# A hybrid encoder layer on one core: sequence mixers stepped between dense products, exponents as sums of clamped differences, and low parts of weights kept in DRAM

## The chip, the cores and the metric

The kernel runs on one core of a Trainium2 chip. The metric is the device time of one execution in microseconds (us), the median of several runs. The engines are named as the profile names them: PE (TensorE), its weight loads PEld, DVE (VectorE), ACT (ScalarE), POOL (GpSimd) and SP (SyncE, whose queue issues all DMAs of this kernel).

## What is computed

One encoder layer is applied to two independent streams with the same weights: S with 512 tokens and R with 1024, both of width 1024 in float32. Cut to what matters here:

```python
u = rmsnorm(x) @ w_in                      # 3088 columns: z, x/B/C, dt, q, k, v
ssd = gated_norm(scan_fwd(...) + scan_bwd(...) + D * xs, silu(z))
att = rmsnorm(dilated_attention(rope(norm(q)), rope(norm(k)), v))
h = x + concat(ssd, att) @ w_out
h = h + cross_attention(rmsnorm(h), rmsnorm(mem))          # 4 heads, 256 memory tokens
y = h + relu(rmsnorm(h) @ w1) ** 2 @ w2
...
# scan, per chunk of 128 tokens, head and direction
seg = a_cs[i] - a_cs[j]                    # a_cs: running sum of dt * A, A < 0
lmat = where(causal, exp(seg), 0)
y_diag = (C @ B.T * lmat) @ (x * dt)
y_off = (C @ carried_state) * exp(a_cs)
```

## The kernel before

**Dense products in three parts.** A float32 product is made of three fp32r products: both factors are split into a rounded high part and a rest, and `mm3` (lines 180 to 183) adds high x high, low x high and high x low. `load_w` (line 163) brings a slab of weights as two halves `raw` of 0.5 MB over SP's queue; ACT rounds each half into `whi` (line 172), and the rest `wlo` is a subtraction (line 173), of the first half on POOL and of the second on DVE. There are two `raw` buffers and three of `whi` and `wlo`. Each slab of `w_in` (12 of them, 256 columns each) is loaded and split once for S and again for R.

**The order of the work.** The program records the stages one after another: norm and `w_in` of S, scan of S (`ssd`), norm of R's first half, q/k/v of S (`w_in_qkv`), attention of S (`att`), norm and `w_in` of R, scan of R, q/k/v of R, attention of R, the keys and values of the memory tokens (`memory`), then `chain` (w_out and cross attention) and `mlp` of S, and the same two of R. A scheduler then orders each engine's instructions: of those whose inputs and buffers it holds to be ready, the one recorded first goes first. So a later stage's dense products already stand between the steps of a mixer that waits. Each engine, and the SP queue, runs its own instructions strictly in that order.

**The scan** (line 463 on). A backward pass makes the states that come from the right and stores them in DRAM. The forward pass takes chunk by chunk (128 tokens): it loads x, B, C, z and the stored state, makes C.B for two groups of heads in PSUM bank b (line 542) and masks it for both directions (DVE, line 545). For each of two groups of four heads it loads rows `se` of the running sums, broadcast to all partitions (line 551), and forms the exponent as the smaller of the two directions' differences:

```python
nc.scalar.activation(e[:, 0, h], e[:, 0, h], AF.Identity, bias=col[0])                       # line 555
nc.vector.scalar_tensor_tensor(e[:, 0, h], w[:, h], col[1], e[:, 0, h], op0=OP.add, op1=OP.min)   # 556
```

Lines 557 and 558 weigh the masked C.B with dt (ACT and DVE), 559 takes Exp (ACT), 560 multiplies (POOL), and 563 applies the result to x in bank c. Two products with the carried states follow (line 573, both in bank b, read by DVE at 575 into `syo`), and the state's own product (line 513, bank b again).

**q, k and v** (line 401 on). For each slab and each pair of token tiles two projections of 24 products each (256 columns) are copied out by ACT (line 448). For q and k, `heads` squares, sums, takes a reciprocal root on POOL (line 190), scales and rotates (DVE and POOL, 421 to 428), and transposes on PE (line 433).

**Attention** (line 619 on). Four pairs of heads; per head a band pattern and a class pattern; units of two query tiles. A unit is scores in bank a (line 653), the mask and maximum on DVE (655), Exp on ACT (660), transposes in bank b (666), a copy, and values in bank c (676).

## Time and profile before

| | |
|---|---|
| three runs | 2495.92, 2488.87, 2497.25 us; median 2495.92 |
| the profiled execution | 2489.01 us, span of its instructions 2487.2 us |
| mean granted clock of TensorE | 0.993 |
| busy, share of the span | PE 97%, DVE 56%, ACT 38%, POOL 28% |
| DMA | 272.6 MB in all |

An instruction's line in the profile is the line of the function that records it: all dense products stand under lines 181 to 183, and the name of the tile tells them apart (`mm` and `tp` are banks of dense products and transposes, `ma`, `mb`, `mc` the three banks of the mixers). A name ends in s or p where it belongs to S or R (`acs`, `acp`). The span falls into stretches by what runs: up to about 70 us the start and w_in of S, to 212 the scan of S with q/k/v of S, to 447 attention of S with w_in of R, to 756 the scan of R with q/k/v of R and the memory products and the first part of attention R, to 1132 the rest of attention R with memory and the chain of S, and from there the MLP of S and all else of R.

### The profile page before, as it was taken

Reading aid. Unit: us, or ns where it says so; the run is one execution under the profiler, and the core shown is the slowest. Engines: PE = TensorE matmul, PEld = TensorE weight load, DVE = VectorE, ACT = ScalarE, POOL = GpSimd, SP = SyncE. Lnnn points to the kernel's source line nnn. Section 1 sums busy time; section 2 is a strip of 40 time slices with the busy share of each in tenths; the row PEclk is TensorE's granted clock in tenths of the full one; section 3 lists DMA queues with packets and bytes.
Section 4 is the critical chain, followed back from the end, with each engine's and each line's share of the span. In section 5 each row is a group of like instructions: output and inputs, shape, how many; then the busy total and the mean of one; then the engine's idle time right before and its main releaser. Section 6 shows DMA issues by size and latency. Waiting matters only on the chain.

```text
span 2487.2 us, 43450 instructions
## 1 busy us (share of the span) xinstructions
PE 2419.2 (97%) x17363; PEld 2268.0 (91%) x17363; DVE 1394.9 (56%) x2750; ACT 951.3 (38%) x2153; POOL 698.4 (28%) x492
## 2 busy tenths in 40 slices
PE   8989999999989999999999999999999999999999
PEld 8889999889889988999989999999989989989897
DVE  6896775787735666655445636445544444443444
ACT  6655554455544655543222315334412212112120
POOL 3363112564422221314334211111222222122220
PEclk9999999999999999999999999999999999999999
DMA  5755443765567253425233411111111111101101
GB/s 187 243 192 181 126 146 106 225 201 189 187 194 214 85 150 98 116 83 184 92 101 103 170 52 35 52 60 44 35 52 35 51 52 51 52 35 52 52 35 68
DMA packets 224059, 272.59 MB, mean 110 GB/s; under 512 B 39634, under 2 KB 178160, under 8 KB 223856
## 3 DMA queue, kind: packets, MB, share of 16 engines
q1 hardware_dynamic: 223856, 269.80, 34.1%
q8 instruction: 137, 2.24, 0.4%
q14 instruction: 66, 0.54, 0.1%
HBM read 215.55 MB, written 54.20 MB: 108 GB/s over the span
## 4 chain that ended last, share of the span: by engine, by line
PE 79%; DMA 6%; DVE 6%; issue 3%; POOL 2%; ACT 2%; SPq 1%; POOLq 0%; DVEq 0%; ACTq 0%
PE mm L181 16%; PE mm L183 16%; PE mm L182 16%; PE tp L183 7%; PE tp L182 7%; PE tp L181 7%; PE mc L676 2%; PE ma L653 2%; PE mb L666 1%; DMA se<-acp 1%; DVE wlo L173 1%; PE tp L199 1%; DVE se L558 1%; POOL wlo L173 1%; DMA ak<-qkp 1%
## 5 line engine op out<-in xcount | busy, mean ns | idle before, releaser
L181 PE MATMUL mm<-whi,chi 128*128 128x256 f32 x1792 | 516.6, 289 | 2.1 <-ACT mm L749 1.2
L183 PE MATMUL mm<-whi,clo 128*128 128x256 f32 x1792 | 512.2, 287 | 0.0
L182 PE MATMUL mm<-wlo,chi 128*128 128x256 f32 x1792 | 511.3, 286 | 0.0
L947 DVE TENSOR_TENSOR h<-mm,h 128x512 f32<-128x512 f32 x384 | 262.2, 689 | 408.6 <-PE mm L183 408.6
L173 POOL TENSOR_TENSOR wlo<-raw,whi 128x1024 fp32r<-128x1024 f32 x120 | 296.9, 2474 | 601.4 <-ACT whi L172 585.9
L183 PE MATMUL tp<-chi,wlo 128*128 128x256 f32 x1440 | 408.4, 284 | 0.0
L182 PE MATMUL tp<-clo,whi 128*128 128x256 f32 x1440 | 407.9, 283 | 0.0
L181 PE MATMUL tp<-chi,whi 128*128 128x256 f32 x1440 | 405.6, 282 | 0.0
L172 ACT CAST whi<-raw 128x1024 fp32r<-128x1024 f32 x240 | 241.7, 1047 | 293.1 <-PE mm L183 168.1
L181 PEld LDWEIGHTS mm<-whi,chi 128*128 128x128 f32 x1792 | 341.1, 190 | 4.5 <-ACT chi L205 1.7
L182 PEld LDWEIGHTS mm<-wlo,chi 128*128 128x128 f32 x1792 | 341.0, 190 | 1.2 <-issue 0.2
L183 PEld LDWEIGHTS mm<-whi,clo 128*128 128x128 f32 x1792 | 339.9, 190 | 0.4
L173 DVE TENSOR_TENSOR wlo<-raw,whi 128x1024 fp32r<-128x1024 f32 x120 | 265.8, 2215 | 108.5 <-ACT whi L172 108.2
L181 PE MATMUL mm<-whi,hidh 128*128 128x512 f32 x768 | 303.1, 395 | 0.2 <-DVE h L947 0.2
L182 PE MATMUL mm<-wlo,hidh 128*128 128x512 f32 x768 | 302.6, 394 | 0.0
L183 PE MATMUL mm<-whi,hidl 128*128 128x512 f32 x768 | 302.3, 394 | 0.2 <-POOL hidl L932 0.2
L181 PEld LDWEIGHTS tp<-chi,whi 128*128 128x128 f32 x1440 | 272.5, 189 | 8.7
L183 PEld LDWEIGHTS tp<-chi,wlo 128*128 128x128 f32 x1440 | 271.7, 189 | 7.0
L182 PEld LDWEIGHTS tp<-clo,whi 128*128 128x128 f32 x1440 | 270.9, 188 | 6.5
L932 POOL TENSOR_TENSOR hidl<-hr,hidh 128x512 fp32r<-128x512 f32 x96 | 133.3, 1390 | 473.6 <-ACT hidh L931 473.6
L931 ACT CAST hidh<-hr 128x512 fp32r<-128x512 f32 x96 | 59.5, 620 | 320.6 <-PE mm L182 249.6
L183 PEld LDWEIGHTS mm<-whi,hidl 128*128 128x128 f32 x768 | 144.3, 188 | 34.0 <-POOL hidl L932 0.6
(283 smaller groups left out, 4398.3 us busy)
## 6 DMA issues: line engine op xcount, KB each, us to landing
raw<-in_mlp_w_dram SPq DMA_DIRECT2D x128, 512.0 KB
raw<-in_w_in_dram SPq DMA_DIRECT2D x48, 512.0 KB
qkp<-ev SPq DMA_DIRECT2D x32, 256.0 KB
se<-acp SPq DMA_DIRECT2D x16, 512.0 KB
raw<-in_xatt_wkv_dram SPq DMA_DIRECT2D x16, 512.0 KB
ak<-qkp SPq DMA_DIRECT2D x32, 256.0 KB
raw<-in_w_out_dram SPq DMA_DIRECT2D x16, 512.0 KB
raw<-in_xatt_wq_dram SPq DMA_DIRECT2D x16, 512.0 KB
```

The source lines that it names most:

```text
L172: nc.scalar.copy(hi[:, sl, :], raw)
L173: (nc.vector if s else nc.gpsimd).tensor_tensor(lo[:, sl, :], raw, f(hi[:, sl, :]), op=OP.subtract)
L181: nc.tensor.matmul(ps, lh, rh, start=start, stop=False)
L182: nc.tensor.matmul(ps, lh, rl, start=False, stop=False)
L183: nc.tensor.matmul(ps, ll, rh, start=False, stop=stop)
L199: nc.tensor.transpose(pt[:, k, t, :], xn[t][:, (2 * kp + k) * 128:(2 * kp + k + 1) * 128], units(2 * kp + k))
L558: nc.vector.scalar_tensor_tensor(w[:, h], cbm[:, 0, g], col[2], w[:, h], op0=OP.mult, op1=OP.add)
L653: nc.tensor.matmul(pq[:, i, :W], qu, ops[i][0][j], start=j == 0, stop=j == 1)
L676: nc.tensor.matmul(po[:, i * 64:i * 64 + 64], pT[:, i * nk + j, :], ops[i][1][j][:, rs], start=j == 0, stop=j == nk - 1)
L931: nc.scalar.copy(hh[:, ft], r)
L932: nc.gpsimd.tensor_tensor(hl[:, ft], r, f(hh[:, ft]), op=OP.subtract)
L947: nc.vector.tensor_tensor(h[t][:, cs], ps, h[t][:, cs], op=OP.add)
```

## The change

**Kept rests.** `load_w` takes a key, which only slabs of w_in have. The first time a slab with a key is split (for S), both halves of the rest are made by POOL and the whole rest is stored to DRAM; the second time (for R) it is loaded from there instead of being made again. Other weights are split as before.

**Exponents.** The exponent is minus the sum of the two directions' differences, each clamped at zero by a Relu on ACT; POOL adds them, and ACT takes Exp with scale -1.

**Weaving.** The stages become generators that yield after a step: a mixer after a part of a chunk or a unit, a dense stage after one projection bank or pair of tiles. `weave` takes `rate` mixer steps for each dense step, so the recorded order itself alternates. In the scan, the loads, the masks and the weights of chunk c+1 are recorded during chunk c, the state's product and one of the two products with carried states use bank a. In q/k/v the transposes of a pair of tiles are recorded after the next pair's projections; in `xbc` those of the convolution likewise. In attention a unit's scores, transposes and values are recorded in three successive steps, so three units are under way. Attention R is woven into `memory`, `chain` of S and `mlp` of S.

```diff
+    def load_w(src, a, b, key=None):
...
+            if kept is not None:
+                nc.sync.dma_start(f(lo[:, sl, :]), kept[:, sl, :])
+            else:
+                eng = nc.gpsimd if key or s == 0 else nc.vector
+                eng.tensor_tensor(lo[:, sl, :], raw, f(hi[:, sl, :]), op=OP.subtract)
+        if key and kept is None:
+            rests[key] = tc.dram_tile([128, a, b], F32, name="rest%d" % len(rests))
+            nc.sync.dma_start(rests[key], f(lo))
...
-                    nc.scalar.activation(e[:, 0, h], e[:, 0, h], AF.Identity, bias=col[0])
-                    nc.vector.scalar_tensor_tensor(e[:, 0, h], w[:, h], col[1], e[:, 0, h], op0=OP.add, op1=OP.min)
...
+        def weigh(c, g, cbm, e):
+            w = e[:, 1]
+            for h in range(4):
+                for d in range(2):
+                    col = acs[:, c, d * 8 + g * 4 + h:d * 8 + g * 4 + h + 1]
+                    nc.scalar.activation(e[:, d, h], e[:, d, h], AF.Relu, scale=-1.0, bias=col)
+            nc.gpsimd.tensor_tensor(e[:, 0], e[:, 0], w, op=OP.add)
+            nc.scalar.activation(e[:, 0], e[:, 0], AF.Exp, scale=-1.0)
+            for h in range(4):
+                col = [st.dt[:, c, d * 8 + g * 4 + h:d * 8 + g * 4 + h + 1] for d in range(2)]
+                nc.scalar.activation(w[:, h], cbm[:, 1, g], AF.Identity, scale=col[1])
+                nc.vector.scalar_tensor_tensor(w[:, h], cbm[:, 0, g], col[0], w[:, h], op0=OP.mult, op1=OP.add)
+            nc.gpsimd.tensor_tensor(w, w, e[:, 0], op=OP.mult)
...
+        def outside(c, d, prev, y):
...
+            po = mx_bank("ab"[d])
...
+            inside(c, 0, py)
+            if nxt:
+                tiles[c + 1] = load(c + 1, True)
+                e0 = rows_of(c + 1, 0)
+                xs = decayed(x, c, 0)
+            yield
+            inside(c, 1, py)
+            if nxt:
+                cbm = masks(c + 1)
+                e1 = rows_of(c + 1, 1)
             nc.vector.tensor_tensor(y, py, y, op=OP.add)
+            outside(c, 0, carry, y)
+            yield
+            if nxt:
+                weigh(c + 1, 0, cbm, e0)
+            outside(c, 1, pb, y)
...
+            yield
+            if nxt:
+                carry = update(carry, xs, bt, c, 0)
+                weigh(c + 1, 1, cbm, e1)
...
+                if behind:
+                    transposed(*behind.pop())
                 if c < 4:
                     heads(c, t, hl)
+                    behind.append((c, t, hl))
...
+    def weave(mixer, rate, dense):
+        due = 0.0
+        for _ in dense:
+            due += rate
+            while due >= 1.0:
+                due -= 1.0
+                next(mixer, None)
...
+            mixer = ssd(S, mp)
+            weave(mixer, 1.5, w_in_norm(R, pool, atB, 0))
+            rot = rotations(pool)
+            weave(mixer, 1.7, w_in_qkv(S, pool, rot))
+            run(mixer)
...
+            mixer = att(S, mp)
+            weave(mixer, 1.6, w_in_norm(R, pool, atA, 1))
+            weave(mixer, 1.6, w_in(R, pool, wx))
+            run(mixer)
...
+            mixer = ssd(R, mp)
+            weave(mixer, 1.8, w_in_qkv(R, pool, rot, lambda: memory_norm(pool, atB)))
+            run(mixer)
...
+        mixer = att(R, att_pool.__enter__())
+        weave(mixer, 1, memory(pool, lambda: [mix_T(S, pr, atA) for pr in range(2)]))
...
+        weave(mixer, 1, chain(S, (atA,), hp, tp_only))
...
+            weave(mixer, 1, mlp(S, hid, lambda: [run(mixer)] + [mix_T(R, pr, atA) for pr in range(2)]))
```

Three places of the orders that the two programs get show what moves.

On SP's queue, at the second and third slab of w_in in S's pass (`raw` is half a slab, `wd` the columns of dt), before:

```order
L171 DMA raw_470<-in_w_in_dram 128x4x256
L171 DMA raw_474<-in_w_in_dram 128x4x256
L346 DMA wd_4053<-in_w_in_dram 128x8x16
L171 DMA raw_620<-in_w_in_dram 128x4x256
L171 DMA raw_624<-in_w_in_dram 128x4x256
```

and after the change:

```order
L175 DMA raw_464<-in_w_in_dram 128x4x256
L184 DMA rest0_254<-wlo_245 128x2048
L175 DMA raw_468<-in_w_in_dram 128x4x256
L371 DMA wd_3273<-in_w_in_dram 128x8x16
L175 DMA raw_616<-in_w_in_dram 128x4x256
L184 DMA rest1_472<-wlo_463 128x2048
L175 DMA raw_620<-in_w_in_dram 128x4x256
```

The store of a slab's rest stands between the two loads of the next slab; it waits for POOL's second subtraction, as the load behind it does, which takes that half's buffer.

On PE, in the scan of R, one chunk from its products with carried states to the next chunk's masks ("..." stands for dense products, `tp` for q/k transposes), before:

```order
L573 MATMUL mb_5931<-carry_5850,sbc_5867 128x256 x2
...
L563 MATMUL mc_5879<-sx_5863,se_5880 128x64 x4
L573 MATMUL mb_5937<-spb_5871,sbc_5867 128x256 x2
L563 MATMUL mc_5879<-sx_5863,se_5904 128x64 x4
...
L513 MATMUL mb_5945<-sxs_5943,sbt_5865 128x256 x2
...
L542 MATMUL mb_5971<-sbc_5965 128x128 x2
```

and after the change:

```order
L551 MATMUL ma_6954<-sxs_6819,sbt_6482 128x256 x2
...
L607 MATMUL mc_6806<-sx_6480,se_6577 128x64 x4
L616 MATMUL mb_6946<-spb_6804,sbc_6484 128x256 x2
L616 MATMUL ma_7098<-carry_6957,sbc_6815 128x256 x2
...
L463 MATMUL tp_7158<-tab_75,ev_6990 128x128 x4
...
L576 MATMUL mb_7089<-sbc_7079 128x128 x2
L463 MATMUL tp_7297<-tab_75,ev_7105 128x128 x4
L607 MATMUL mc_7070<-sx_6811,se_6817 128x64 x4
```

All four products of a chunk other than the inner one used bank b in turn; now two of them use bank a, and the product with the carried state already belongs to the next chunk.

On POOL, in the same scan (`rsr` is a reciprocal root, `ev` a rotation of q or k, `se` a group's exponents and weights), before:

```order
L560 TENSOR_TENSOR se_5684<-se_5684 128x512
L565 TENSOR_TENSOR sy_5830<-sx_5765,rowt_76 128x512
L560 TENSOR_TENSOR se_5708<-se_5708 128x512
L190 TENSOR_TENSOR rsr_7365<-rst_7363,nhalf_79 128x8
L426 TENSOR_TENSOR ev_7306<-ev_7307,rot_1705 128x64 x2
L576 TENSOR_TENSOR sy_5732<-sy_5732,syo_5738 128x512
```

and after the change:

```order
L594 TENSOR_TENSOR se_6229<-se_6229 128x512
L452 TENSOR_TENSOR ev_6613<-ev_6614,rot_1326 128x64 x2
L594 TENSOR_TENSOR se_6320<-se_6320 128x512
L557 TENSOR_TENSOR carry_6693<-carry_6440,sdec_5579 128x512
L600 TENSOR_TENSOR se_6229<-se_6229 128x512
L202 TENSOR_TENSOR rsr_6793<-rst_6791,nhalf_79 128x8
L619 TENSOR_TENSOR sy_6214<-sy_6214,syo_6345 128x512
L600 TENSOR_TENSOR se_6320<-se_6320 128x512
```

Each group now has two operations there, the sum (line 594) and the product (line 600), and others stand between them.

## Rows read from the trace of the kernel before

**Rows 1.** The page: span, and PE's busy time, share and instructions.

```profile
span 2487.2 us, 43450 instructions
...
PE 2419.2 (97%) x17363; PEld 2268.0 (91%) x17363; DVE 1394.9 (56%) x2750; ACT 951.3 (38%) x2153; POOL 698.4 (28%) x492
```

**Rows 2.** Busy time in one stretch of 50 us; columns as in rows 3.

```profile
200.00:250.00 50.00, 50.00 (x433) 49.28 (x433) 30.44 (x92) 30.02 (x76) 10.60 (x11) 1.00 0.53 173
```

**Rows 3.** Busy time by stretch: from:to, length, then the header's columns.

```profile
core 0: us, PE busy (x) PEld busy (x) DVE busy (x) ACT busy (x) POOL busy (x), PEclk, DMA share, GB/s
0.00:70.00 70.00, 60.38 (x487) 58.56 (x488) 48.22 (x109) 41.59 (x71) 20.05 (x19) 1.00 0.61 194
70.00:212.00 142.00, 130.08 (x1014) 126.05 (x1013) 120.67 (x241) 79.93 (x187) 77.32 (x63) 0.96 0.66 214
212.00:447.00 235.00, 232.36 (x1986) 230.20 (x1985) 152.97 (x446) 121.68 (x319) 50.48 (x41) 1.00 0.45 136
447.00:756.00 309.00, 280.63 (x2178) 271.08 (x2178) 212.24 (x479) 155.30 (x420) 147.24 (x125) 0.97 0.63 200
756.00:1132.00 376.00, 366.81 (x2790) 347.48 (x2789) 224.95 (x576) 193.07 (x515) 97.08 (x57) 1.00 0.42 120
1132.00:2487.00 1355.00, 1348.93 (x8920) 1234.65 (x8918) 635.82 (x903) 359.68 (x645) 306.22 (x188) 1.00 0.19 66
```

**Rows 4.** Waits of PE over the span: total us, times, longest.

```profile
PE tp L433 <- DVE ev L428: 11.9, 7, 3.2
...
PE ma L653 <- DMA ak<-qkp: 5.4, 3, 2.8
PE mb L573 <- DVE syo L575: 5.1, 2, 4.4
PE ma L653 <- DVE aband L655: 4.3, 4, 2.7
```

**Rows 5.** Stretches at half clock: the first of seven, and their sum.

```profile
82.00:88.60 6.60, 4.76 (x18) 4.23 (x19) 6.58 (x20) 4.52 (x15) 0.00 (x0) 0.50 0.58 212
...
sum 28.20, PE 25.86 PEld 23.94 DVE 18.72 ACT 10.39 POOL 9.06; mean PE 3.69 PEld 3.42 DVE 2.67 ACT 1.48 POOL 1.29
```

**Rows 6.** Line 173 alone, by stretch: DVE busy, POOL busy, clock, DMA.

```profile
70.00:212.00 142.00, 16.38 (x9) 22.21 (x9) 0.96 0.66 214
...
447.00:756.00 309.00, 22.61 (x12) 30.72 (x12) 0.97 0.63 200
```

**Rows 7.** Line 173: durations of one, ns, minimum/median/maximum, and first and last start.

```profile
L173 POOL TENSOR_TENSOR wlo<-raw,whi x120: 2347/2407/3412, 13.1 to 2422.7; 128x1024 fp32r<-128x1024 f32 x120
L173 DVE TENSOR_TENSOR wlo<-raw,whi x120: 1154/2522/3407, 15.1 to 2423.3; 128x1024 fp32r<-128x1024 f32 x120
```

**Rows 8.** Groups: busy us, mean ns of one | idle before, releasers.

```profile
L190 POOL TENSOR_TENSOR rsr<-rst,nhalf 128x8 f32<-128x8 f32 x25 | 42.4, 1695 | 38.5 <-DVE rst L188 37.9
L556 DVE SCALAR_TENSOR_TENSOR se<-se,sa 128x128 f32<-128x128 f32 x96 | 35.7, 415 | 9.8 <-ACT se L555 9.7
L560 POOL TENSOR_TENSOR se<-se 128x512 f32<-128x512 f32 x24 | 32.3, 1350 | 14.6 <-DVE se L558 12.0 <-issue 1.0 <-PE mc L563 0.8
L555 ACT ACTIVATE se<-se,sa 128x128 f32<-128x128 f32 x96 | 30.7, 390 | 33.8 <-DMA se<-acp 26.6 <-DMA se<-acs 5.6 <-POOL ev L426 1.6
```

**Rows 9.** Line 556 alone, by stretch: DVE busy, clock, DMA.

```profile
70.00:212.00 142.00, 11.50 (x32) 0.96 0.66 214
...
447.00:756.00 309.00, 24.18 (x64) 0.97 0.63 200
```

**Rows 10.** Waits of PE in 70 to 212 us, the longest three.

```profile
PE tp L433 <- DVE ev L428: 5.3, 3, 2.1
PE tp L199 <- DVE sdd L478: 2.7, 1, 2.7
PE ma L483 <- DVE sacs L474: 1.8, 1, 1.8
```

**Rows 11.** Waits of PE in 447 to 756 us, the longest.

```profile
PE tp L433 <- DVE ev L428: 6.7, 4, 3.2
```

More of the change, by code (lines that the diff above doesn't have):

```diff
@@ L167, in load_w @@
         h = a // 2
+        kept = rests.get(key)
         for s in range(2):
@@ L385, in steps @@
             nc.vector.scalar_tensor_tensor(st.dt, q, 2.0, v, op0=OP.mult, op1=OP.add)
+            yield
         for part, i in ((xbc, 0), (steps, 0), (xbc, 1), (xbc, 2), (xbc, 3), (gate, 0), (gate, 1)):
-            part(i)
+            yield from part(i)
     def rotations(pool):
@@ L458, in w_in_qkv @@
                     mid()
+                yield
     def ssd(st, pool):
@@ L525, in ssd, with masks @@
             x, bt = load(c, False)
[L526 removed]
+            xs = decayed(x, c, 1)
+            yield
+            carry = update(carry, xs, bt, c, 1)
             nc.sync.dma_start(st.pb[c - 1], carry)
[L529 to L539 removed]
+        tiles, weights = {}, {}
+        def masks(c):
+            bc = tiles[c][2]
             pcb = mx_bank("b")
@@ new lines, in inside @@
+        def inside(c, g, py):
+            w, x = weights.pop((c, g)), tiles[c][0]
+            for h in range(4):
+                hs = slice((g * 4 + h) * 64, (g * 4 + h) * 64 + 64)
+                nc.tensor.matmul(py[:, hs], w[:, h], x[:, hs], start=True, stop=True)
+        def outside(c, d, prev, y):
+            if prev is None:
+                return
+            bc = tiles[c][2]
+            po = mx_bank("ab"[d])
+            for g in range(2):
+                gs = slice(g * 256, g * 256 + 256)
+                nc.tensor.matmul(po[:, gs], bc[:, 2 + g, :], prev[:, gs], start=True, stop=True)
+            t = pool.tile([128, 512], F32, name="syo", bufs=1)
+            nc.vector.tensor_tensor(h3(t), h3(po), bc64(eacs[:, c, d * 8:d * 8 + 8]), op=OP.mult)
+            nc.gpsimd.tensor_tensor(y, y, t, op=OP.add)
@@ L564, in ssd @@
+        tiles[0] = load(0, True)
+        yield
+        carry = None
+        cbm = masks(0)
+        for g in range(2):
+            weigh(0, g, cbm, rows_of(0, g))
+            yield
+        for c in range(nt):
+            nxt = c + 1 < nt
+            sl = slice(c * 128, c * 128 + 128)
+            x, bt, bc = tiles[c]
             y = pool.tile([128, 512], F32, name="sy", bufs=2)
             nc.gpsimd.tensor_tensor(h3(y), h3(x), bc64(Dsk), op=OP.mult)
-            nc.vector.tensor_tensor(y, py, y, op=OP.add)
@@ L567, in ssd @@
-            for d in range(2):
-                if prev[d] is None:
-                    continue
-                po = mx_bank("b")
-                for g in range(2):
-                    gs = slice(g * 256, g * 256 + 256)
-                    nc.tensor.matmul(po[:, gs], bc[:, 2 + g, :], prev[d][:, gs], start=True, stop=True)
-                t = pool.tile([128, 512], F32, name="syo", bufs=1)
-                nc.vector.tensor_tensor(h3(t), h3(po), bc64(eacs[:, c, d * 8:d * 8 + 8]), op=OP.mult)
-                nc.gpsimd.tensor_tensor(y, y, t, op=OP.add)
@@ L683, in part, with step @@
                     nc.sync.dma_start(out[r], no[:, i])
+            return [(u0, (scores, transposed, values)) for u0 in range(0, nt, 2)]
+        flying = []
+        def step(unit):
+            if unit:
+                flying.append((*unit, 0, ()))
+            for i, (u0, stages, n, r) in enumerate(list(flying)):
+                flying[i] = (u0, stages, n + 1, stages[n](u0, *r))
+            if flying and flying[0][2] == 3:
+                flying.pop(0)
         for h in range(2):
@@ L687, in att_pair @@
             for classes in (False, True):
-                part(h, classes, qs, ks)
+                for unit in part(h, classes, qs, ks):
+                    step(unit)
+                    yield
+        while flying:
+            step(None)
+            yield
         cls = pool.tile([128, nt, 2, 66], F32, name="acl", bufs=1)
@@ L957, in mlp, with run @@
             nc.sync.dma_start(st.y[t * 128:t * 128 + 128, :], h[t])
+    def run(gen):
+        for _ in gen:
+            pass
+    def weave(mixer, rate, dense):
[5 more added lines that the diff above has]
+                next(mixer, None)
     tp_only = lambda tag: tp_bank()
@@ L975, in hm @@
             st.hm.append(norm_h(st, pr, pools[pr // 2], "mlp_norm_g", banks))
-        w_out(st, hp, hn)
+        yield from w_out(st, hp, hn)
         with tc.tile_pool(name="xa" + st.tag, bufs=1, reuse_waits="tile") as xp:
-            xattn(st, xp, xp, bank, lambda: hn(last), hm)
+            yield from xattn(st, xp, xp, bank, lambda: hn(last), hm)
     with ExitStack() as es:
```

150 lines of the change are left out of this document (75 added, 75 removed).

## The prediction

> **What bounds the kernel now.** I read the views in this order: busy shares, the table of stretches, the waits of TensorE, and the groups on the lines that the change touches. PE is busy 2419.2 of 2487.2 us [rows 1], so only what keeps PE from its next product counts. An undisturbed stretch runs 433 matmuls in 50 us [rows 2], 0.116 us each; nothing in the change alters how many dense products there are, so that part stays. The stretches [rows 3] show where PE is kept waiting. Its idle time is 142 - 130.1 = 11.9 us in 70 to 212 (the scan of the short stream S between its q/k/v products), 2.6 in 212 to 447 (attention S, w_in of R), 28.4 in 447 to 756 (the scan of R, then the start of attention R) and 9.2 in 756 to 1132 (attention R between memory and chain S): 52.1 us together. In the first stretch DVE is busy 120.7 of 142 us, 85%; in the third 212.2 of 309, the most loaded engine after PE in both. From 1132 on, no mixer runs and PE idles 6.1 us in 1355. The waits [rows 4] name the same places: the q/k transposes behind DVE's rotation 11.9 us, the scan's one PSUM bank b behind DVE 5.1, the score products behind their loads of K 5.4 and behind DVE 4.3. [...]
>
> **The change, part by part.** The sum stands against the profiled execution, 2489.0 us, span 2487.2. The three runs shown have a median of 2495.9, from 2488.9 to 2497.3, so the profiled one lies at their low end.
>
> *Kept rests.* Twelve slabs of w_in are used by S and again by R. In S's pass DVE loses its 12 halves to POOL; in R's pass the 24 subtractions go, and 24 loads of 0.5 MB come; 12 stores of 1 MB are new in S's pass. Of these DVE loses 9 in 70 to 212, 16.4 us, and POOL, which has 9 of its own there, gains 9 x 2.41 = 21.7 [rows 6, 7]. In R's q/k/v products both lose about 5 of the 12 halves shown in 447 to 756: 5/12 of 22.6 and 30.7 us, 9.4 on DVE and 12.8 on POOL [rows 6]. The stores bring 12.6 MB into the first 212 us, 59 GB/s above 194 and 214 at a DMA share of 0.61 and 0.66 [rows 3]; in proportion the share rises to about 0.83. Below 1 I cost this at 1 us, with bounds of 0 (the weights are three buffers deep) and 10 (a late half slab of 48 products, 5.6 us, twice). The store waits on the SP queue for POOL's second half, and behind it stands the raw load that waits for the same subtraction anyway; the next loads of the scan stand further back, and they are what pays if POOL is late. At the very start, the first slab's second half now waits for the first on POOL, 2.4 us, where DVE took it alongside: 1 us, bounds 0 and 2.4.
>
> *Exponents.* Per group of four heads, 4 DVE operations of 0.37 us busy go (96 in all, 35.7 us: 11.5 and 24.2 in the two scans [rows 8, 9]), 4 more ACT operations of 0.32 come, and one more POOL operation like the 1.35 us product. POOL's sum now stands in the middle of the chain: ACT, POOL, ACT and DVE, POOL.
>
> *The loads that result.* In 70 to 212 DVE goes from 120.7 to 120.7 - 16.4 - 11.5 = 92.8, 65%; POOL from 77.3 to 77.3 + 21.7 + 8 x 1.35 = 109.8, 77%, and is the most loaded there; ACT reaches 79.9 + 10.2, 63%. In 447 to 756 DVE goes to 212.2 - 9.4 - 24.2 = 178.6, 58%; POOL to 147.2 - 12.8 + 21.6 = 156, 50%; ACT to 155.3 + 20.5 = 176, 57%. No engine beside PE keeps 85%.
>
> *Weaving: scan.* A chunk's exponent rows are loaded half a chunk before ACT needs them; before, ACT sat idle 26.6 + 5.6 us behind these loads [rows 8]. The state product and one of the two outer products move from bank b to bank a, so a chunk uses bank b twice instead of four times, and the 5.1 us behind syo lose their cause. The q/k transposes stand after the next pair of projections in the code, but counted in the scheduler's order this is less: 98 dense products behind their own projection on average, 85 before, so 13 x 0.116 = 1.5 us more cover, while the waits were 7 of 1.7 us on average. Of the 11.9 us in 70 to 212, where three waits ended by DVE make 9.8 [rows 10], I take 7: DVE has a quarter less to do, but POOL now feeds the same chains; bounds 0 and 11.9. Of the 28.4 in 447 to 756 I take 13: bank b 5.1, half of the transposes' 6.7 there [rows 11], and 4.6 of the smaller DVE waits; bounds 0 and 25.
>
> *Weaving: attention.* Scores, transposes and values of a unit are three steps apart, and attention R is spread from the memory products into the MLP of S, so that more dense products lie between its parts. The loads of K and q are issued as before. Of the 2.6 + 9.2 us I take 5, bounds 0 and 10.
>
> [...]
>
> *The sum.* 7 + 13 + 5 + 7 - 1 - 1 = 30 us, 2489 - 30 = 2459 us for a run like the profiled one. The median of runs lay 6.9 us above it before, so I put the median of the changed kernel at **2460**.
>
> [...] DVE's subtraction takes 1154 ns at best and 2522 in the median, up to 3407, while POOL's stays at 2347 to 3412 with a median of 2407 [rows 7]: something in POOL's half makes DVE's half wait. [...]
>
> **The rivals.**
> [...]
> - *The order hardly changes.* The scheduler wove already: 85 against 98 products. Then attention's 5 us, the transposes' 3.3 and half of the clock term go: 2459 + 12 = 2471.
> - *POOL takes DVE's place.* 77% on an engine whose operations last 1.35 to 2.4 us, with the reciprocal roots of q and k in the same queue. Then scan S wins nothing, scan R only bank b (13 becomes 5), the clock 2: 2459 + 7 + 8 + 5 = 2479, the median near 2486.
> - *Slower: ACT stands behind POOL's sum.* The Exp waits at the head of ACT's queue for the new sum, and the copies that free the three PSUM banks of the dense products queue behind it. A bank lasts 24 products, 2.8 us, so PE stalls once ACT is held for more than two banks, 5.6 us. With a subtraction (2.4), a sum of the other group (1.35), one root (1.7 us [rows 8]) and the sum itself (1.35), POOL's queue holds 6.8: 1.2 us too long, and 24 groups make 29 us, with nothing won in the scans or the clock: 2489 - 5 + 2 + 29 = 2515. Against it: subtractions are gone in R's pass, and the scheduler places other ACT work ahead of the Exp.
>
> **How the numbers follow.** Forecast 0.50, port 0.08, order 0.15, POOL 0.17, slower 0.10. The range reaches from 2432, where the large terms come near their upper bounds and the costs to nothing (11 + 23 + 9 + 14 = 57 us below 2489), to 2492, which holds the first four cases with the 7 us between the profiled run and the median; it leaves out the slower case and the far end of the gain, some 0.15 together. A measurement of this kernel can tell about 0.3%, 7.5 us. Faster by more: the first three cases and a little of the fourth, 0.76; within 0.3%: 0.14; slower: 0.10.
>
> **What would show it.** DVE busy falls by some 80 us (24 subtractions of 1.8 to 1.9 [rows 6] and the 35.7), POOL's busy time stays within 20 us, ACT's rises by 30. In the scan stretches PE's idle time falls from 40 to about 20 us; the wait of bank b behind syo is gone; clock places at 0.50 fall from seven to three or four. From some 1132 us on, little changes but attention R's instructions. I am wrong if PE's waits move to POOL's product or to ACT's copies in the scans with the same total, if raw loads or kept rests appear among PE's waits, or if PE idles as long as before with DVE a third lighter.

## The result: 0.66% slower, and the profile after

The changed kernel takes 2512.8 us in the median of four runs (2505.3 to 2513.8), beside 2494.7 for the kernel before, also in four (2488.9 to 2497.3). The ratio is 1.0066, 95% interval 1.0046 to 1.0086: slower. The forecast was 2460, and 2432 to 2492 the range. The profiled execution of the changed kernel took 2505.3 us, 7.6 below its median; that of before stood 5.7 below, so the two can be set side by side. Differences of a few us between them are still within what executions of one kernel differ by.

The page of the changed kernel, its span and its busy times:

```profile
span 2503.5 us, 43408 instructions
...
PE 2424.7 (97%) x17363; PEld 2272.5 (91%) x17363; DVE 1356.8 (54%) x2628; ACT 976.9 (39%) x2249; POOL 715.6 (29%) x516
```

TensorE runs the same 17,363 matmuls as in [rows 1]. DVE has 122 instructions fewer and is busy 38 us less. PE, for whose sake that was done, is idle 2503.5 - 2424.7 = 78.8 us, where it was 68.0, and busy 5.5 us longer for the same matmuls, which I put down to its clock (0.992 granted in the mean, 0.993 in before; more below). Those two make the 16.3 us of longer span.

Busy time of the changed kernel by stretch, columns as in rows 3:

```profile
core 0: us, PE busy (x) PEld busy (x) DVE busy (x) ACT busy (x) POOL busy (x), PEclk, DMA share, GB/s
0.00:70.00 70.00, 59.65 (x463) 57.40 (x463) 51.90 (x102) 40.16 (x69) 32.74 (x23) 1.00 0.76 250
70.00:212.00 142.00, 123.52 (x957) 119.88 (x956) 99.31 (x187) 86.60 (x211) 91.66 (x73) 0.95 0.83 276
212.00:447.00 235.00, 230.59 (x1970) 228.29 (x1969) 131.99 (x422) 121.81 (x319) 25.11 (x29) 1.00 0.54 164
447.00:756.00 309.00, 282.96 (x2201) 273.80 (x2200) 196.46 (x433) 172.62 (x486) 163.93 (x143) 0.97 0.67 210
756.00:1132.00 376.00, 362.94 (x2669) 340.89 (x2668) 220.94 (x490) 174.19 (x434) 97.56 (x59) 0.99 0.43 124
```

The line to look at is the second. DVE fell from 85% of the scan of S [rows 3] to 70%, and PE's idle time there rose from 11.9 us to 142 - 123.5 = 18.5. In the scan of R (fourth line) DVE fell from 69% to 64% and PE's idle time from 28.4 to 26.0 only. In the other three stretches it rose by 0.7, 1.8 and 3.9. The stretches are fixed in time while the work in them shifts, but the reading holds without them: from a scan's first state product to its last inner product PE idles 7.5 us in before (85.6 to 197.0) and 14.3 in the changed kernel (106.8 to 213.2) for S, and 20.4 (448.9 to 662.8) and 17.9 (470.7 to 652.0) for R.

PE's waits in the changed kernel: total us, times, longest.

```profile
PE ma L551 <- DVE syo L618: 9.5, 2, 8.1
...
PE tp L463 <- DVE ev L454: 4.5, 5, 1.9
PE ma L737 <- DVE aband L739: 4.1, 4, 1.2
PE mm L193 <- ACT ev L480: 3.9, 1, 3.9
PE tp L193 <- DVE xpT L977: 3.7, 1, 3.7
PE tp L349 <- DVE cacc L338: 3.6, 2, 2.0
PE mb L576 <- issue: 3.5, 2, 3.2
PE mm L193 <- ACT mm L857: 3.4, 3, 2.1
PE mc L607 <- POOL se L600: 3.4, 3, 2.6
PE mm L193 <- DVE ev L362: 3.2, 2, 2.6
PE mb L616 <- issue: 3.0, 1, 3.0
```

Against [rows 4]: the q/k transposes behind the rotation went from 11.9 us to 4.5, as foretold, and the loads of R's K from 5.4 to 0.7 (further down). But the wait behind syo, which was to lose its cause with bank b, stands on top with 9.5, now in bank a: 8.1 in the scan of S and 1.4 in that of R, where the 5.1 of before were. The rest is a list of waits of 3 to 4 us that were smaller or absent in before: ACT's evictions, the convolution's transposes, the products with xpT, and two rows named "issue", for which the view knows no releaser. Both of these are bank b behind DVE again (start, length, engine, line, operation, in brackets the idle time before it):

```profile
138.96 0.74 DVE L579 TENSOR_TENSOR scbm<-mb,tab 128x256 f32<-128x256 f32 x2
139.80 1.18 PE L616 MATMUL mb<-spb,sbc 128*128 128x256 f32 x4 [3.02 <-issue]
...
557.05 3.41 DVE L181 TENSOR_TENSOR wlo<-raw,whi 128x1024 fp32r<-128x1024 f32 x1
...
563.58 0.68 DVE L618 TENSOR_TENSOR syo<-mb,seacs 128x512 f32<-128x512 f32 x1
564.36 1.20 PE L576 MATMUL mb<-sbc 128*128 128x128 f32 x4 [3.18 <-issue]
```

The loads were there in time: spb had landed at 134.15 and sbc at 558.80, by the updates of their semaphores. PE starts right after DVE has read bank b, at 139.70 and 564.26. In the second case syo stood behind a subtraction that took 3.41 us beside one on POOL, where the shortest on DVE takes 1.21 in this kernel; 563.94 to 570.77 us is then a place at half clock.

The places at half clock, summed over the nine that the changed kernel has before its last microseconds:

```profile
sum 40.95, PE 34.45 PEld 33.57 DVE 27.91 ACT 24.80 POOL 20.41; mean PE 3.83 PEld 3.73 DVE 3.10 ACT 2.76 POOL 2.27
```

That is 40.95 us in nine places after 28.20 in seven [rows 5]. In them the next 128x256 product starts 0.213 us after the last in the median, elsewhere 0.120. By my estimate from these two the 12.75 us more cost some 5.6; PE's busy time, 5.5 us longer, fits that.

The largest wait, from the same timeline:

```profile
144.87 1.08 PE L616 MATMUL ma<-carry,sbc 128*128 128x256 f32 x4
...
146.01 2.10 DVE L232 TENSOR_SCALAR xn<-xn,rsr 128x1024 f32<-128x1024 f32 x1
...
149.96 0.16 DVE L200 TENSOR_SCALAR rst<-qss 128x8 f32<-128x8 f32 x1
150.59 2.44 ACT L593 ACTIVATE se<-se,sacs 128x128 f32<-128x128 f32 x8 [1.87 <-DMA se<-acs]
...
151.89 0.69 DVE L447 TENSOR_TENSOR ev<-ev,rsr 128x512 f32<-128x512 f32 x1 [1.77 <-POOL rsr L202]
152.94 0.61 ACT L665 ACTIVATE syo<-sy 128x512 f32<-128x512 f32 x1
...
153.68 0.15 DVE L200 TENSOR_SCALAR rst<-sss 128x1 f32<-128x1 f32 x1 [1.10 <-ACT syo L665]
153.75 0.68 DVE L618 TENSOR_TENSOR syo<-ma,seacs 128x512 f32<-128x512 f32 x1
...
154.48 2.07 PE L551 MATMUL ma<-sxs,sbt 128*128 128x256 f32 x4 [8.08 <-DVE syo L618]
```

PE needs bank a for the next state product (L551). The product with the carried state (L616) has filled the bank by 145.95, but its eviction by DVE (syo, L618) starts at 153.75, 7.8 us later. What stands ahead of syo in DVE's queue fills that time. Until 150.12 DVE works without a pause, 4.2 us: a norm of R (L232), the copy of a transpose, the sums of q's squares and the gate, up to L200. Then it waits 1.77 us for POOL's root of q, takes 0.69 for the product with that root, and waits 1.10 for ACT's Square (L665). Only this last part leads back to a load: the first load of se is issued at 143.37 and has landed at 150.22, ACT stands 1.87 us at their first use until 150.59, and the Square comes behind those eight operations in ACT's queue. So about 5 of the 7.8 us are DVE's own work in the order that the scheduler gave it, 1.8 are POOL's root and 1.1 a late load. PE lost 8.08, and 150.93 to 157.76 us is one of the places at half clock.

### The profile page after: what moved, and what is told of

Read it like the earlier page. It is cut to its first block, busy times and chain, and to the rows that moved or that the text cites. A ratio compares the mean times of both kernels' runs of the same rounds, so it can differ in the third digit from the quotient of the medians.

```text
span 2503.5 us, 43408 instructions
## 1 busy us (share of the span) xinstructions
PE 2424.7 (97%) x17363; PEld 2272.5 (91%) x17363; DVE 1356.8 (54%) x2628; ACT 976.9 (39%) x2249; POOL 715.6 (29%) x516
## 4 chain that ended last, share of the span: by engine, by line
PE 68%; DMA 5%; DVE 3%; ACT 2%; issue 2%; POOL 1%; SPq 0%; POOLq 0%; DVEq 0%; ACTq 0%
PE mm L193 13%; PE mm L194 13%; PE mm L195 13%; PE tp L194 7%; PE tp L195 7%; PE tp L193 7%; PE mc L766 2%; PE ma L737 1%; PE mb L753 1%; PE tp L211 1%; DMA se<-acp 1%; DMA xn<-mixp 1%; DMA nclp<-ano 0%; DVE wlo L181 0%; PE tp L934 0%
## 5 line engine op out<-in xcount | busy, mean ns | idle before, releaser
L181 POOL TENSOR_TENSOR wlo<-raw,whi 128x1024 fp32r<-128x1024 f32 x120 | 290.3, 2421 | 547.2 <-ACT whi L176 537.7
L176 ACT CAST whi<-raw 128x1024 fp32r<-128x1024 f32 x240 | 242.0, 1047 | 278.2 <-PE mm L195 150.5
L181 DVE TENSOR_TENSOR wlo<-raw,whi 128x1024 fp32r<-128x1024 f32 x96 | 228.8, 2384 | 84.0 <-ACT whi L176 84.0
```

The costliest lines, as they stand in the source:

```text
L176: nc.scalar.copy(hi[:, sl, :], raw)
L181: eng.tensor_tensor(lo[:, sl, :], raw, f(hi[:, sl, :]), op=OP.subtract)
```

## The experiments

Eighteen more kernels were run. Medians are of 4 to 12 runs, each beside 11 to 35 runs of before on the same chip, with medians of 2497.2 to 2498.1; the change itself has its four runs from above, so every difference against it is uncertain by some 5 us. "us" is the ratio less one times 2498; idle is the span less PE's busy time. Those two are of one profiled execution, which for most lies near the median of its kernel; before's and the change's lie some 9 and 8 below theirs.

| kernel | what it is | median | ratio [95%] | us | PE idle | PE busy |
|---|---|---|---|---|---|---|
| before | | 2497.2 to 2498.1 | | | 68.0 | 2419.2 |
| rests_only | before + kept rests | 2511.3 | 1.0049 [1.0035, 1.0063] | +12 | 75.8 | 2434.6 |
| exp_only | before + exponents | 2525.4 | 1.0105 [1.0088, 1.0122] | +26 | 83.3 | 2441.0 |
| rests_exp | before + both | 2541.2 | 1.0166 [1.0150, 1.0181] | +41 | 94.1 | 2445.6 |
| weave_only | weaving alone | 2507.4 | 1.0038 [1.0025, 1.0050] | +9 | 77.4 | 2429.1 |
| weave_exp | weaving + exponents | 2502.4 | 1.0018 [1.0007, 1.0028] | +4 | 74.5 | 2426.1 |
| weave_rests | weaving + rests | 2516.1 | 1.0069 [1.0055, 1.0082] | +17 | 80.1 | 2431.5 |
| after | all three | 2512.8 | 1.0066 [1.0046, 1.0086] | +16 | 78.8 | 2424.7 |
| rests_split | after, DVE's halves kept in S | 2514.6 | 1.0062 [1.0047, 1.0077] | +15 | 85.1 | 2432.1 |
| halves_only | after, POOL's halves, nothing kept | 2518.3 | 1.0076 [1.0063, 1.0090] | +19 | 87.5 | 2430.9 |
| rests_late | after, stores issued later | 2509.3 | 1.0045 [1.0031, 1.0058] | +11 | 81.4 | 2426.1 |
| null_rot | before, another order | 2499.9 | 1.0008 [1.0000, 1.0017] | +2 | 70.2 | 2422.3 |
| null_kq | before, another order | 2495.3 | 0.9982 [0.9974, 0.9991] | -4 | 70.2 | 2423.0 |
| att_r_first | weave_exp, attention R unwoven | 2499.4 | 1.0003 [0.9995, 1.0012] | +1 | 68.3 | 2430.1 |
| scan_r_first | weave_exp, scan R unwoven | 2503.1 | 1.0017 [1.0007, 1.0028] | +4 | 80.9 | 2424.0 |
| exp_sum_dve | exp_only, sum on DVE | 2510.1 | 1.0052 [1.0039, 1.0066] | +13 | 75.8 | 2431.5 |
| weave_sum_dve | weave_exp, sum on DVE | 2506.0 | 1.0034 [1.0018, 1.0050] | +8 | 82.4 | 2426.3 |
| before_dve | before, two scan operations on DVE | 2489.9 | 0.9965 [0.9952, 0.9978] | -9 | 69.8 | 2418.3 |
| after_dve | after, the same two on DVE | 2506.7 | 1.0028 [1.0015, 1.0041] | +7 | 77.4 | 2427.5 |
| before_dve_kq | before_dve and null_kq | 2493.2 | 0.9987 [0.9978, 0.9995] | -3 | 67.9 | 2426.4 |

PE's busy time, for the same 17,363 matmuls, is lowest in the rows with little idle time and highest in rests_exp with the most: the kernels that make PE wait more mostly have its clock fall more too (granted in the mean 0.981 in rests_exp, 0.985 in exp_only and 0.993 in before, though 0.992 in scan_r_first with 80.9 us of idle time). Of the 37.1 us between the profiled executions of exp_only and before, 15.3 are idle time and 21.8 longer busy time.

### The parts, alone and together

The change without kept rests (weave_exp, the first two lines), with the old exponents (weave_rests, the rest), and without both (weave_only):

```diff
-        key = ("w_in", c0) if w is W_IN else None
+        key = None
...
-                    nc.scalar.activation(e[:, d, h], e[:, d, h], AF.Relu, scale=-1.0, bias=col)
+                nc.scalar.activation(e[:, 0, h], e[:, 0, h], AF.Identity, bias=col[0])
+                nc.vector.scalar_tensor_tensor(e[:, 0, h], w[:, h], col[1], e[:, 0, h], op0=OP.add, op1=OP.min)
```

> The changed kernel without kept rests (w_in's rests made again for R, second halves on DVE). Theory rests: the 18 us that the change lost come from the stores (DMA share 0.83 in 70 to 212 us) and from POOL making both halves in S's pass, where the changed kernel fell 10 to 15 us behind by its 800th dense product; then this one returns to 2495 us or a little below. Theory weave: the new order of the mixers made the loss; then this one stays at 2505 to 2515. Theory exponents: the same, 2505 to 2515.

> The changed kernel with the old exponents (one Identity on ACT and one minimum on DVE per head, no sum on POOL). Theory exponents: POOL's sum in the middle of the chain delays the scans; then the loss goes, 2490 to 2498 us. Theories rests and weave: 2508 to 2518, a little slower than the changed kernel where DVE is the loaded one.

> Only the weaving of the three parts: old exponents and no kept rests. Theory weave: 2505 to 2515 us, the loss is here. Theory rests: below 2495, since the smaller waits of PE in the scans and in attention remain. Theory exponents: below 2495 too.

The kernel before with the kept rests and the exponents (the same lines put in), and with one of them:

> The kernel before with kept rests and the new exponents, no weaving. Theory weave: this one has DVE's relief without the new order, 2475 to 2490 us. Theory rests: 2505 to 2515. Theory exponents: 2500 to 2510.

> The kernel before with kept rests alone. Without weaving, kept rests and exponents together cost 43 us; with weaving kept rests cost 9 to 10 and the exponents give 3 to 5 back. Theory rests (stores and POOL's halves in S's pass hurt, more where the mixers stand packed): 2530 to 2540, nearly all of the 43. Theory exponents (POOL's sum in the chain hurts where a chunk is not prepared ahead): 2505 to 2512, as with weaving.

> The kernel before with the new exponents alone. Theory exponents: 2520 to 2535, since without the chunk ahead ACT, POOL, ACT, DVE and POOL stand in one chain before the inner product. Theory rests: 2493 to 2500.

Kept rests cost in any company: +12 alone, +15 beside the exponents (41 - 26), +8 beside weaving (17 - 9), +12 beside both (16 - 4). The exponents cost +26 on the kernel before, and -5 or -1 once the scan is woven. Weaving alone costs +9. So no part paid, two of three cost something of their own, and the only gain is that weaving takes away the price of the exponents.

Weaving was to shorten the wait of the q/k transposes; in weave_only that row reads

```profile
PE tp L463 <- DVE ev L454: 17.8, 13, 2.9
```

where before had 11.9 in 7 [rows 4]. In the planned order more products stand between projection and transposes, and DVE was late all the same. That the scan's steps in DVE's queue held the rotations up is likely, but not shown.

### Kept rests: transfers, POOL's halves, or SP's queue

rests_split lets DVE make the second halves in S's pass again; halves_only leaves POOL both halves there and makes the rests again for R, with no store and no load:

```diff
-                eng = nc.gpsimd if key or s == 0 else nc.vector
+                eng = nc.vector if s else nc.gpsimd
```

```diff
-            if kept is not None:
-                nc.sync.dma_start(f(lo[:, sl, :]), kept[:, sl, :])
-            else:
-                eng = nc.gpsimd if key or s == 0 else nc.vector
-                eng.tensor_tensor(lo[:, sl, :], raw, f(hi[:, sl, :]), op=OP.subtract)
+            eng = nc.gpsimd if first or s == 0 else nc.vector
+            eng.tensor_tensor(lo[:, sl, :], raw, f(hi[:, sl, :]), op=OP.subtract)
```

> The changed kernel, but in S's pass DVE makes the second half of each rest as before; stores and loads stay. Theory POOL's halves: POOL's queue in S's pass is what hurts; 2500 to 2505, as without kept rests. Theory stores: the DMA traffic of the 12 stores makes the scan's loads late; 2510 to 2516, unchanged.

> The changed kernel, with both halves on POOL in S's pass, but nothing stored; R's pass makes its rests again, on POOL and DVE. Theory POOL's halves: 2508 to 2516. Theory stores: 2500 to 2505, and the DMA share of 70 to 212 us back at 0.66.

Either half of the idea alone costs as much as the whole: +15 and +19 beside +16, all against +4 without any. So neither the transfers nor POOL's load can be named as the cause by itself; each is enough.

The traces show one thing that is common to both halves. In the eight kernels that have either of them, the scan of S runs its first state product behind 576 to 616 dense products, at 98.0 to 107.9 us; in the other twelve it stands behind 456, at 83.3 to 87.3 us. PE's order is planned before the run, so it is the scheduler that starts the scan later there. From 0 to 440 us PE then idles more than in the same kernel without rests: by 14.7 us in rests_only, 7.6 in rests_exp, 9.0 in weave_rests and 5.3 in the change. That the later start is the price is not shown, since no run changes it alone.

The queue of SP was a third suspect. Its waits from 0 to 212 us in the changed kernel (total us, times, longest):

```profile
SPq L184 <- POOL wlo L181: 19.9, 8, 6.0
SPq L175 <- POOL wlo L181: 17.7, 9, 6.2
```

rests_late issues each store when the next weights are loaded:

```diff
-            nc.sync.dma_start(rests[key], f(lo))
+            put_off.append((rests[key], f(lo)))
```

> The change, with each store of a kept rest issued when the next weights are loaded, behind their loads, instead of right behind its own product; same transfers, same work. Theory E (SP's queue: in the changed kernel SP stands 20 us at the stores of the rests, waiting for POOL's product, while the scan's and the convolution's transfers are queued behind): back to the version without kept rests, so -6 to -14 us against the change (2499 to 2507 beside a before of 2498). Rival F (the 24 MB more of transfers, or POOL's second halves, cost by themselves): within +-4 us of the change.

It takes 5 us off, the least of what theory E asked for being 6, and not clear of the change's own uncertainty. SP no longer stands at the stores, but more at the loads of the raw weights (L176 there), whose buffers wait for the same products of POOL:

```profile
SPq L176 <- POOL wlo L182: 28.4, 13, 5.7
```

So 37.6 us became 28.4. The version without kept rests (weave_exp) has almost as much for the subtractions, 16.8 behind POOL's and 9.7 behind DVE's. SP's extra hold was nearly gone, and at most 5 of the 12 us with it. So it may be a part of the price; the larger part stays unassigned.

### How far another order alone moves the time

In null_rot the four products of the rotation are written in another order:

```diff
-            for j, src in enumerate((t1, t2, t1, t2)):
+            for j, src in ((2, t1), (1, t2), (0, t1), (3, t2)):
```

> The kernel before with the four small products of the rotation (L423 to L424 of before) written in the order 2, 1, 0, 3 instead of 0, 1, 2, 3: no work is added, removed or moved between engines, the planner only emits a few instructions in another order. Theory A (each part of the change has a price of its own: kept rests +10 to +14 us, weaving +10 us): 0 +- 3 us, since nothing is paid here. Theory B (the order the planner gave the kernel before was a lucky one, and any edit that makes it plan again costs some 10 us through stalls elsewhere): +5 to +15 us, with the PE's idle time in places that the edit does not touch.

In null_kq the two loads of K stand ahead of the load of q in each head.

> The kernel before with the four loads of K issued ahead of the load of q in each head of the attention (L586 to L590 of before): the same loads, the same work, but the planner's order of TensorE's instructions differs in many places. Theory A (parts have prices of their own): 0 +- 3 us, at most a few us in the attention stages. Theory B (any new order costs some 10 us against a lucky one): +5 to +15 us, with TensorE's lost time outside the attention too.

+2 and -4: theory B falls as an account of +10 and more, but differences up to some 5 us between kernels whose order differs are not evidence.

### What weaving does to attention R and scan R

```diff
-        weave(mixer, 1, memory(pool, lambda: [mix_T(S, pr, atA) for pr in range(2)]))
+        run(mixer)
+        run(memory(pool, lambda: [mix_T(S, pr, atA) for pr in range(2)]))
```

> weave_exp (weaving and new exponents, no kept rests) with the attention of R handed over in full before the memory's products instead of one step after each of them; its pipelining inside a head stays. Theory C (the loss at the end is put off attention work: weave_exp was some 20 us ahead of before at the 5800th dense product and 14 us behind that at the end): -8 to -15 us against weave_exp, so 2487 to 2495 beside a before of 2497. Theory B (orders differ by chance): within +-10 us of weave_exp on either side, with the changes not confined to the stretch after the memory's products.

```diff
-            weave(mixer, 1.8, w_in_qkv(R, pool, rot, lambda: memory_norm(pool, atB)))
-            run(mixer)
+            run(mixer)
+            run(w_in_qkv(R, pool, rot, lambda: memory_norm(pool, atB)))
```

> weave_exp with the scan of R handed over in full before the products of q, k and v of R, as before's code did, instead of 1.8 steps after each pair of them; the scan's inner order (exponents a chunk ahead) stays. Theory D (the weaving's fixed rate in the scan of R is what costs: the woven scan lost 24 us between dense products 2800 and 3400 in weave_only): -5 to -15 us against weave_exp, gained between dense products 2800 and 3800. Theory B (order by chance): within +-10 us on either side. If the weaving of the scan is what makes the new exponents cheap (they cost +28 us alone and -5 us with weaving): +5 to +20 us.

Against weave_exp they make -3 and 0 us, within what order alone moves, so theories C and D fall. The 0 also says that the weaving of R's scan into the dense products is not what makes the new exponents cheap there; what is left is the scan's own order, a chunk ahead, which was not tested alone. att_r_first tells where attention's expected gain went: counted at the same dense product of the profiled executions, it is 45 us behind weave_exp at the 5400th, 5 at the 6600th and 2 ahead at the last. Weaving puts attention's work off into the MLP of S, looks faster until then, and pays it back in full.

### The hand-over to POOL

```diff
-                nc.gpsimd.tensor_tensor(e[:, 0], e[:, 0], w, op=OP.add)
+                nc.vector.tensor_tensor(e[:, 0], e[:, 0], w, op=OP.add)
```

> exp_only (before with the new exponents alone, +28 us over before) with their sum on VectorE instead of POOL. Theory H (the added hop over POOL, 1.34 us and two hand-overs in each of the 24 chains that the unwoven scan waits for, is the price): -12 to -25 us against exp_only. Rival A (ScalarE's four more operations of 0.39 us for each chain, 37 us in all, in front of which its evictions stand): within +-5 us of exp_only.

> weave_exp (weaving, new exponents, no kept rests) with the sum of the two differences (L594 of after) on VectorE instead of POOL: 24 operations of about 1.3 us go from POOL, 24 of about 0.7 us come to VectorE. Theory P (POOL's two-operand work stretches VectorE's operations that run beside it: in the traces every VectorE operation that takes over 0.1 us more than its form's quick ones overlaps POOL's work, some 205 to 230 us in all, 15 of them at L594): VectorE's load stays about as it was (+17 of work, -15 of stretch), the chain to the exponential is shorter, and the time falls by 3 to 8 us against weave_exp. Rival L (VectorE's load is what PE waits for): +3 to +8 us.

On the unwoven scan half of the exponents' price, 13 of 26 us, was the sum's turn on POOL (theory H). Little of that is PE's own wait behind POOL's product. In exp_only and then in exp_sum_dve:

```profile
PE mc L564 <- POOL se L561: 6.0, 3, 3.8
```

```profile
PE mc L564 <- POOL se L561: 2.7, 2, 2.2
```

Woven, the same edit gives +4, not told from order alone; there the groups are made a chunk ahead. before_dve and after_dve move the product of exponential and weights and the addition of syo from POOL to DVE:

```diff
-                nc.gpsimd.tensor_tensor(w, w, e[:, 0], op=OP.mult)
+                nc.vector.tensor_tensor(w, w, e[:, 0], op=OP.mult)
...
-                nc.gpsimd.tensor_tensor(y, y, t, op=OP.add)
+                nc.vector.tensor_tensor(y, y, t, op=OP.add)
```

> The kernel before with two of the scan's POOL operations on VectorE: the product of exponential and weights (L560, 24 of 1.35 us) and the addition of syo to y (L576, 22 times). Theory P (POOL's work stretches VectorE's beside it, by 20 us at these two lines in before): VectorE's load rises by some 12 us only, chains shorten, 0 to -6 us against before. Rival L (VectorE's load is what PE waits for, it is 92% busy at 70 to 212 us): +5 to +15 us.

> The changed kernel with the product of exponential and weights (L600) and the addition of syo to y (L619) on VectorE, as before_dve had them on the kernel before (-8 us there). Theory P (the handing-over to POOL and POOL's interference are a cost in both kernels): -4 to -10 us against the change, so 2503 to 2509 beside a before of 2498. Rival W (in the woven scan the groups are made a chunk ahead, so that POOL's turn is hidden and only VectorE's load is left to count, as the +4 us of weave_sum_dve hints): 0 to +6 us against the change.

They make -9 us on before and -9 on the change (the latter with some 6 us of uncertainty), although DVE gets the work, where rival L asked for +5 to +15. DVE was 85% busy in 70 to 212 us, not the 92% that this rival names [rows 3]. The stretches of before_dve, to be read beside [rows 3]:

```profile
70.00:212.00 142.00, 130.91 (x1013) 126.92 (x1013) 117.40 (x254) 80.03 (x186) 57.10 (x49) 0.95 0.68 217
447.00:756.00 309.00, 281.74 (x2210) 272.03 (x2209) 221.32 (x516) 157.31 (x422) 105.61 (x98) 0.98 0.64 202
```

In the scan of S, DVE has 13 operations more than in before and is busy 3.3 us less; POOL has 20 us less. In the scan of R, DVE has 37 more and is busy 9.1 us more; POOL has 42 us less. The trace does not show where the 9 us were won: PE idles 69.8 us in this profiled execution and 68.0 in that of before, which ran 9 us below its median.

The last run joins the two edits that gained:

> before_dve (the two operations of the scan on VectorE, -8 us against before) with the loads of K ahead of the load of q (null_kq, -3 us against before), the candidate for the fastest version. If the two gains add: 2486 to 2489 beside a before of 2498. If null_kq's -3 us was only another order of the planner: 2487 to 2494, no better than before_dve beyond +-4 us.

They do not add: -3, where before_dve alone had -9. Read the other way, the same two operations moved to DVE on null_kq (-4) give +1. So the edit made -9, -9 and +1 us on three kernels, and differences of 5 us are not evidence; that DVE gains more from POOL's absence than it loses by the work is not shown. before_dve is the fastest kernel found, clearly ahead of the change and ahead of before by 0.35% [0.22%, 0.48%], of which order alone may be a part.

## Why the prediction was wrong

The working had the direction of the loads right, their sizes only in part, and their worth wrong. Point by point:

- *Loads.* Foretold for 70 to 212 us: DVE 92.8, POOL 109.8, ACT 90, DMA share 0.83; found 99.3, 91.7, 86.6, 0.83. For 447 to 756: DVE 178.6, POOL 156, ACT 176; found 196.5, 163.9, 172.6. Two counts of slabs were wrong. Of the nine halves in 70 to 212 three belong to R, which POOL does not take over and where it loses its own three, so POOL was to reach 77.3 + 3 x 2.41 + 10.8 = 95.3. And of the 12 halves in 447 to 756 two are of w_in and not five (before issues the last loads of w_in at 473 us), which gives POOL 163.7.
- *DVE over the span.* It lost the 96 operations on se and 24 subtractions, 83 us of durations, with "some 80" foretold. But all its durations together fell from 1528 to 1476 us, by 52 only: the operations that stayed took 31 us more, the convolution's 120 on cacc 8.8 of it (97.0 to 105.8). The last section has about as much: what they took more beside POOL rose by 30 us, from 184 to 214.
- *Scan S, "Of the 11.9 us in 70 to 212 I take 7: DVE has a quarter less to do".* This is the first step that failed: idle time rose by 6.6. The waits I had named did shrink (the transposes in this stretch from 5.3 [rows 10] to 1.9), but I took a wait that DVE ends for a wait that DVE's load over the stretch makes. What came instead is the wait of 8.08 us above, longer than the whole rise: an eviction behind 5 us of other work in DVE's queue, POOL's root and ACT's Square.
- *Bank b, "the 5.1 us behind syo lose their cause".* The outer product and the state product now share bank a, and PE waited there for the same eviction, 9.5 us. The wait moved with the bank, and mostly to the scan of S; for bank b PE still waited 3.0 and 3.2 us.
- *Scan R, 13.* Found 2.4. The transposes gave more than the 3.3, 6.7 [rows 11] to 2.6, and the wait behind syo 3.7, but behind ACT's evictions PE now waited 3.9 and 3.4 (the latter 1.2 in before), for bank b at the masks' product 3.5 and behind POOL's product 3.4 (2.0 in before).
- *Attention, 5.* Found -5.7 (1.8 and 3.9 lost). Weaving moved the work to chain S and the MLP, and att_r_first shows the same end without it.
- *Clock, 7.* No run shows this term, half of 14.1 us, my upper estimate for the 28.2 us at half clock [rows 5]. Found -5.5, PE's longer busy time, with 40.95 us in nine places instead of seven: the stalls were not fewer. In the 5 us ahead of each of the nine PE idled 1.9 to 4.5 us, ahead of the seven in before 2.1 to 3.9.
- *Kept rests, "Below 1 I cost this at 1 us", bounds 0 and 10.* They cost 8 to 15 in the four comparisons, where this term and the start together stood at 2, with an upper bound of 12.4. This is the other step that failed. The share of 0.83 was foretold, and the loads are not where PE waits: behind DMA it waits 4.0 us in all, apart from one load at the start, and 8.2 in before. That the scheduler would start the scan of S later was not seen. The start, put at 1 us: at the 400th dense product the change is 5.0 us behind before, weave_exp 1.3, so the rests cost 3.7 there, above the bound of 2.4.
- *The sum.* 2459 for a run like the profiled one and a median 6.9 above it make 2466, not the 2460 that stands there; in the rival on POOL the step is taken (2479 and 2486). It changes nothing in the outcome.
- *The rivals.* "Slower: ACT stands behind POOL's sum" gave 2515, near the 2512.8 found, but that is luck: its mechanism did not decide. In the changed kernel ACT's idle time (last column) before the Exp, L595, is 4.7 us behind POOL in 24 groups together, where it needed more than 5.6 in each, while before the first use of se it is 29.7 behind the loads, in [rows 8] 32.2:

```profile
L593 ACT ACTIVATE se<-se,sacs 128x128 f32<-128x128 f32 x192 | 58.8, 389 | 30.9 <-DMA se<-acp 25.0 <-DMA se<-acs 4.7 <-PE mm L195 1.1
...
L595 ACT ACTIVATE se<-se 128x512 f32<-128x512 f32 x24 | 15.1, 628 | 4.8 <-POOL se L594 4.7
```

  "A chunk's exponent rows are loaded half a chunk before ACT needs them" did not bring the loads earlier for ACT. SP waits 15.3 us in the two scans for the products that free one of the two se buffers (8.7 in before); that a group made ahead holds them longer is my reading, and a third buffer was not tried. *Port*, given 0.08: no run shows what joins the two engines. Measured is that DVE's operations took longer beside POOL's: its subtractions L173 in before 1.15 to 1.23 us in the 12 that had none of POOL's beside them, and 2.56 in the median of the other 108. The 31 us of slower DVE operations and the wait of 3.18 us above, behind a subtraction of 3.41, go with that; how much of the loss it makes is open.

What stays open: why weaving alone costs 9 us, and by what path the rests cost theirs, since transfers and POOL's halves each alone brought about all of it and both go with a later start of the scan. The runs show which parts cost; why is in part argued from the waits of single executions.

## What to carry to other kernels

That PE waits for an engine does not say that the engine has too much to do: before counting its relief as gain, list what stands ahead of the awaited operation in that engine's queue, and look whether the edit touches that. The load over a stretch does not tell it. Test the parts of a change alone and together, since the price of one (the exponents, +26 alone, -5 or -1 in the woven scan) can hang on another, and measure once what a reordering without any other change does, here up to 5 us. DVE's operations also took longer here beside POOL's, by 205 us in all in before and 214 in the change, so a move from DVE to POOL can relieve DVE by less than the work that moves: 83 us of durations went, and all of DVE's together fell by 52.

## What the runs showed of the hardware

One DVE operation on 128x2 numbers took 2.32 us beside an operation of POOL, where the median of its line is 0.17. Durations of L939 in the changed kernel (ns, minimum/median/maximum), the addition in each query of chain S:

```profile
L939 DVE TENSOR_SCALAR xss<-xss x24: 153/169/2316, 853.8 to 1738.8; 128x2 f32<-128x2 f32 x24
```

In before the same addition took 172 ns at most. The long one, in the timeline of the changed kernel:

```profile
959.67 3.34 POOL L818 TENSOR_TENSOR aband<-aband,acl 128x1024 f32<-128x1024 f32 x1
960.71 2.32 DVE L939 TENSOR_SCALAR xss<-xss 128x2 f32<-128x2 f32 x1
...
964.27 0.58 PE L193 MATMUL tp<-xpT,xv 128*128 128x256 f32 x1 [3.75 <-DVE xpT L977]
```

It ends at 963.03, as POOL's ends at 963.01; xpT stands behind it on DVE, PE waits 3.75 us, and 963.30 to 970.13 runs at half clock. POOL's operation belongs to attention R, which weaving brought into chain S. Of the other 23 and of the 24 in before none ran beside POOL. In the profiles of before and of the change, every DVE operation that takes over 0.1 us more than the quick ones of its form (its 10th percentile) overlaps one of POOL; the excess is 205 us and 214. Of the 205, 21 lie on operations that the change removes, so on those that stayed the excess rose from 184 to 214. None of these operations reads a PSUM bank, though 219 and 234 that do begin while POOL is busy for over 0.1 us more.
